# Two small constants move to the top of the left side of SBUF: every large tile on the left starts 64 bytes lower

## The chip, the cores and the metric

The kernel runs on one core of one Trainium2 chip. The metric is the device time of one execution in microseconds. Three runs of the kernel before took 1053.03, 1053.21 and 1053.92 us, so the median is 1053.21 us. The execution that the hardware profiler recorded took 1053.37 us, and the span from its first to its last instruction is 1051.6 us.

## The reference

One decoder block is computed on 1024 tokens of width 1024, in float32: a pre-norm, an input projection that feeds eight heads of forgetting attention and eight groups of chunked spatial gating, an output projection with a residual, and a gated MLP of width 2816 with a causal convolution of three taps between its two matrices, a second residual and a final norm.

```python
xn = rmsnorm(h, norm_mix_g)
proj = xn @ w_in
q, k, v = proj[..., :512], proj[..., 512:1024], proj[..., 1024:1536]
log_f = log_sigmoid(proj[..., 2560:] + b_forget)
att = forgetting_attention(q, k, v, log_f)      # softmax(q k' / 8 + c_i - c_j), causal
uv = gelu(proj[..., 1536:2560])
sg = chunked_spatial_gating(u, vg, gmlp_norm_g, w_spatial, b_spatial)
h = h + concat(att, sg) @ w_out
h = h + conv_ffn(rmsnorm(h, norm_ffn_g), w_up, conv_w, conv_b, w_down)
return rmsnorm(h, norm_final_g)
```

## The kernel before, in words

Every large matrix product is cut in four by a scheme with seven block products instead of eight, whose blocks have names such as A11, S2 and T3, B22. Each float32 operand is split in a high and a low part of type float32r (`split_w`, lines 480 to 487: ACT makes the high part, DVE subtracts it to get the low part), and each product is three float32r matmuls. Nearly all of them are 128x512: 128 rows, 128 columns of the stationary operand, 512 columns of the moving one.

The program has these stages in time: the products of the input projection for u, v and the gate (line 588, to about 104 us), those for q and k (line 737, to about 190 us), the spatial gating and the attention with the output projection of the gated half mixed in (lines 1046 to 1226, to about 380 us), the output projection of the attention and the second norm (lines 1464 to 1500), 22 units of the up projection with convolution and gate (line 1555, about 415 to 836 us), and the down projection with the final norm (line 1743, about 836 to 1044 us).

The order of the work on each engine is not written by hand. A class `Pace` records the instructions, knows which tile lies where in SBUF, gives each a cost, and lists them by due time; the order that it finds is then fixed on each engine. What it knows of places comes from `extent`, which adds up the sizes of the pools of one side from the bottom (left) or from the top (right).

SBUF is used as two stacks of pools. On the left, from the bottom up: `cst` (constants that live to the end), `sml` (small results of the attention), `early` (the tiles of the stages up to the attention: V, H0 to H3, x1, x2, t2, t3, wy, gg). When `early` is released, the pools `upl` (moving blocks xB11, xB21, xT2, xT3, the ring `wha`, the ring `sg`), `xtp`, `pst` and `dn` take its place. On the right, from the top down: `raws` (raw weights) and `late` (A, G0 to G3, pt, whl), later `upr` (xT1, xT4, xB22 and the ring `whb`). The left stack ends at byte 135136 of each partition, where the right one begins: all of it is in use.

The lines that the prediction names are these. Line 533 (ACT) and line 534 (DVE) split the first x tiles: those from tiles H read from byte 32 of the tile on, those from tiles V from byte 0. Line 616 (DVE) subtracts two x tiles. Line 814 is the matmul of the forget gate, whose stationary operand is a slice of 64 columns (256 bytes) of a tile `w` and whose moving operand is an x tile. Lines 1046, 1125 and 1500 are transposes on TensorE, with the constant `ident` as the moving operand. Lines 1555 and 1743 are the matmuls of the up and the down projection. Line 446 is the warm-up.

The two constants of the change are these:

- `lim`, 128x1 float32: set to 3e38 (line 448) and read as the first scalar of the running minimum in the attention (line 1112).
- `bcol`, 64x2 float32: the bias of the forget gate and its negative, read by the small operations of `forget` and `forget_sums`.

Of the kernel before, what the change touches and what calls it, by code (L numbers as in the profile page):

```python
# [8 lines left out]
F32 = mybir.dt.float32  # L9
# [5 lines left out]
P = 128  # L15
# [365 lines left out]
def block_kernel(ctx: ExitStack, tc: tile.TileContext, xT, xtok, wuv, wuw, wv, wqk, wf, cpk, xg, bfv,  # L381
# [3 lines left out]
    pace = Pace(tc)  # L385

    cst = pace.pool(ctx.enter_context(tc.tile_pool(name="cst", bufs=1)))
    sml = pace.pool(ctx.enter_context(tc.tile_pool(name="sml", bufs=1)), ring=4)
    early = pace.pool(tc.alloc_tile_pool(name="early", bufs=1))
    raws = pace.pool(tc.alloc_tile_pool(name="raws", bufs=1, side="right"), "right")  # L390
    late = pace.pool(tc.alloc_tile_pool(name="late", bufs=1, side="right"), "right")
    drm = ctx.enter_context(tc.tile_pool(name="drm", bufs=1, space=bass.MemoryType.DRAM))
# [43 lines left out]
    bs = cp[:, C_BS:C_BS + 8]  # L436
    eo = cst.tile([P, 2], F32, name="eo")
    eps, one = eo[:, 0:1], eo[:, 1:2]
    lim = cst.tile([P, 1], F32, name="lim")
    dve.memset(eps, EPS)  # L440

    warm = nc.const_aps.tensor(1.0, [P, 512], BF16)
# [17 lines left out]
    ng1 = cst.tile([P, 8], F32, name="ng1")  # L460
    rstd1 = cst.tile([P, 8], F32, name="rstd1")
    ss1 = cst.tile([P, 8], F32, name="ss1")
    bcol = cst.tile([64, 2], F32, name="bcol")


    qd = drm.tile([8, 2, 64, 1024], F32, name="qd")
# [923 lines left out]
        wo_split(3, hf, "pool")  # L1390
    ss2 = cst.tile([P, 8], F32, name="ss2")

    early.release()
    upl = pace.pool(tc.alloc_tile_pool(name="upl", bufs=1, reuse_waits="tile"))
    xtp = pace.pool(tc.alloc_tile_pool(name="xtp", bufs=1, reuse_waits="tile"))
# [560 lines left out]
```

## Time and profile before

| What | Value |
|---|---|
| median of three runs | 1053.21 us |
| the profiled execution | 1053.37 us |
| its span | 1051.6 us |
| PE busy | 1044.4 us, 99% of the span |
| DVE busy | 922.5 us, 88% |
| ACT busy | 575.4 us, 55% |
| POOL busy | 251.1 us, 24% |
| DMA, all queues | 158.24 MB, mean 150 GB/s |

PE stands for the matmuls of TensorE, PEld for the loads of its stationary operand, DVE for VectorE, ACT for ScalarE and POOL for GpSimd. [...]

### The profile page before, as it was taken

The page shows a single profiled execution, that of the slowest core. Times are in us where ns is not written, and L with a number is a line of the kernel's source. Part 1 is how long each engine was busy: PE and PEld are TensorE (multiplying, and loading weights), DVE is VectorE, ACT ScalarE, POOL GpSimd, SP SyncE. Part 2 cuts the span into 40 slices and gives each one's busy share as a digit, 9 for nine tenths or more (in the row PEclk, how much of TensorE's full clock was granted, in tenths as well). Part 3 has the DMA queues.
Part 4 walks back from the last instruction along what each step waited for, and adds up shares of the span by engine and source line. Part 5 has one row for each costly group of instructions (what it writes and reads, how often), then busy time and mean ns, then how long its engine had stood idle before and what let it go on. Part 6 is the DMA issues. An engine that isn't in the chain of part 4 may idle for free.

```text
span 1051.6 us, 14304 instructions
## 1 busy us (share of the span) xinstructions
PE 1044.4 (99%) x4925; PEld 866.3 (82%) x4925; DVE 922.5 (88%) x1389; ACT 575.4 (55%) x1007; POOL 251.1 (24%) x212
## 2 busy tenths in 40 slices
PE   9999999999999999999999999999999999999997
PEld 7888788888888888888888888888888888888886
DVE  6987999988888879999999999999998895697775
ACT  6658455477777756645444444444444454454653
POOL 0002243233362250073342433424322000000000
PEclk9999999999999999999999999999999999999999
DMA  9243267865664454214223331332323995333352
GB/s 341 92 149 100 73 183 235 267 213 160 224 208 141 141 186 175 80 66 146 101 90 131 100 138 63 116 125 73 133 75 102 346 388 202 94 98 99 95 180 90
DMA packets 65322, 158.24 MB, mean 150 GB/s; under 512 B 7697, under 2 KB 8537, under 8 KB 65249
## 3 DMA queue, kind: packets, MB, share of 16 engines
q1 hardware_dynamic: 64816, 156.50, 44.7%
q8 instruction: 39, 0.64, 0.3%
q10 hardware_dynamic: 432, 0.82, 0.2%
q14 instruction: 35, 0.28, 0.1%
HBM read 114.98 MB, written 42.31 MB: 150 GB/s over the span
## 4 chain that ended last, share of the span: by engine, by line
PE 99%; DVE 1%; ACT 0%; issue 0%
PE s L1555 23%; PE b L1555 17%; PE s L1743 11%; PE b L1743 9%; PE s L588 6%; PE b L588 5%; PE fl L1226 4%; PE s L737 4%; PE po L1147 3%; PE b L737 3%; PE tr L1125 3%; PE lg L1105 2%; PE lg L1104 2%; PE b L1466 1%; PE b L1465 1%; PE b L1464 1%
## 5 line engine op out<-in xcount | busy, mean ns | idle before, releaser
L1555 PE MATMUL s<-xT,whb 128*128 128x512 f32 x804 | 189.4, 389 | 0.0
L1555 PEld LDWEIGHTS s<-xT,whb 128*128 128x128 f32 x804 | 151.0, 188 | 31.3
L1555 PE MATMUL b<-xB,wha 128*128 128x512 f32 x528 | 126.9, 389 | 0.0
L1743 PE MATMUL s<-whb,wha 128*128 128x512 f32 (+1 forms) x528 | 118.9, 387 | 0.0
L1555 PEld LDWEIGHTS b<-xB,wha 128*128 128x128 f32 x528 | 99.0, 188 | 20.4
L1743 PEld LDWEIGHTS s<-whb,wha 128*128 128x128 f32 x528 | 98.5, 188 | 20.2
L481 ACT CAST whb<-sg 128x512 fp32r<-128x512 f32 x82 | 50.7, 618 | 91.8 <-PE s L1555 82.4
L481 ACT CAST wha<-sg 128x512 fp32r<-128x512 f32 x77 | 47.9, 622 | 92.3 <-PE b L1743 42.1
L1743 PE MATMUL b<-whb,wha 128*128 128x512 f32 (+1 forms) x408 | 91.8, 386 | 0.0
L1743 PEld LDWEIGHTS b<-whb,wha 128*128 128x128 f32 x408 | 75.9, 188 | 15.4
L487 DVE TENSOR_TENSOR wha<-sg,wha 128x512 fp32r<-128x512 f32 x77 | 52.9, 687 | 40.2 <-ACT wha L481 40.1
L1444 POOL TENSOR_TENSOR sg<-raw,raw 128x512 f32<-128x512 f32 x20 | 33.8, 1688 | 162.1 <-DVE whb L487 162.1
L1226 PE MATMUL fl<-whl,H 128*128 128x512 f32 x192 | 63.9, 407 | 0.0
L1147 PE MATMUL po<-pt,V 128*64 128x256 f32 (+6 forms) x240 | 63.9, 343 | 0.0
L1555 PE MATMUL s<-xB,whb 128*128 128x512 f32 x264 | 63.6, 390 | 0.0
L1131 ACT CAST pt<-tr 128x512 fp32r<-128x512 f32 (+2 forms) x96 | 45.2, 478 | 31.8 <-PE tr L1125 20.1
L1555 PE MATMUL b<-xT,whb 128*128 128x512 f32 x252 | 60.7, 389 | 0.0
L487 DVE TENSOR_TENSOR whb<-sg,whb 128x512 fp32r<-128x512 f32 x82 | 57.7, 723 | 2.1 <-ACT whb L481 2.0
L1136 DVE TENSOR_TENSOR pt<-tr,pt 128x512 fp32r<-128x512 f32 (+1 forms) x96 | 52.1, 552 | 7.7 <-ACT pt L1131 7.1
L1555 PEld LDWEIGHTS s<-xB,whb 128*128 128x128 f32 x264 | 49.5, 188 | 10.6 <-DVE h L1626 0.3
L1442 POOL TENSOR_TENSOR sg<-raw 128x512 f32<-128x512 f32 x20 | 41.5, 2076 | 60.0 <-DMA raw<-wup 58.0
L1555 PEld LDWEIGHTS b<-xT,whb 128*128 128x128 f32 x252 | 47.3, 188 | 9.8
(381 smaller groups left out, 2306.9 us busy)
## 6 DMA issues: line engine op xcount, KB each, us to landing
raw<-wup SPq DMA_DIRECT2D x44, 512.0 KB, 3.7
sg<-hx SPq DMA_DIRECT2D x77, 256.0 KB, 2.7
hx<-hs SPq DMA_DIRECT2D x44, 256.0 KB, 3.6
hx<-ca SPq DMA_DIRECT2D x33, 256.0 KB, 2.3
xT<-wdn SPq DMA_DIRECT2D x28, 256.0 KB, 5.4
raw<-wqk SPq DMA_DIRECT2D x8, 512.0 KB, 3.9
kd<-G SPq DMA_DIRECT2D x16, 256.0 KB, 5.1
qd<-G SPq DMA_DIRECT2D x16, 256.0 KB, 3.6
```

The source lines that it names most:

```text
L481: act.copy(h, src)
L487: return eng.tensor_tensor(out=l, in0=src, in1=f32(h), op=ALU.subtract)
L588: pe.matmul(banks[m], xs(n, xi, k)[:, ms], w[:, wi, :], start=(first and k == 0 and c == 0), stop=(k == 3 and c == 2), skip_group_check=True)
L737: pe.matmul(ps, w[:, wi, ks], xs(n, xi, k), start=(first and c == 0), stop=(c == 11), skip_group_check=True)
L1131: act.copy(pt[:, 0, o:512], ps[:, o:512])
L1136: dve.tensor_tensor(out=pt[:, 1, o:512], in0=ps[:, o:512], in1=f32(pt[:, 0, o:512]), op=ALU.subtract)
L1147: pe.matmul(po[0:n, c:e], lhs[:, 0:n], pt[:, s, c:e], start=(k == 0 and s == 0), stop=(k == 4 * hf + 3 and s == 1), skip_group_check=True)
L1226: pe.matmul(self.bank, sgT[k][:, xi, ts_], self.w[hf, k][:, wi, :], start=(k == 0 and i == 0), stop=(k == 3 and i == 2))
L1442: pool.tensor_tensor(out=s[0], in0=a21, in1=a22, op=ALU.add)
L1444: pool.tensor_tensor(out=s[2], in0=a21, in1=a11, op=ALU.add)
L1555: pe.matmul(ps, w[:, wi, ks], xb[:, xi, k, :], start=(first and n == 0), stop=(n == 11), skip_group_check=True)
L1743: pe.matmul(banks[bk + m if at is None else at][:, cs], xh[:, xi, ms], wh[:, wi, cs], start=((first and p_ == 0 or at == 0 and p_ == NP - ...
```

## The change

A pool `tiny` is opened on the left, on top of `early`. `lim` and `bcol` are taken from it instead of from `cst`, and it is released just ahead of `early`. Each of the two takes 32 bytes of a partition, so everything above `cst` on the left lies 64 bytes lower, and what lies in `cst` between and above the two lies 32 or 64 bytes lower.

| Tile | start before (modulo 512) | start now (modulo 512) |
|---|---|---|
| `lim` | 1952 (416) | 135072 (416) |
| `bcol` | 3360 (288) | 135104 (448) |
| `ident` | 1984 (448) | 1952 (416) |
| first tile of `early`, V; later xB11 | 4064 (480) | 4000 (416) |
| every other large tile on the left | (480) | (416) |
| x data within H0, first and second row | (0) and (32) | (448) and (480) |
| first tile of `late`, G0 | 135136 (480) | 135136 (480) |
| every other large tile on the right | (480) | (480) |

The instructions of each engine, their order, their shapes, and the semaphores and values that they wait for and raise are the same in both programs; what differs are the addresses of the operands on the left. Large tiles are multiples of 512 bytes long, so all tiles of a side share one remainder.

```diff
@@ -387,6 +387,7 @@
     cst = pace.pool(ctx.enter_context(tc.tile_pool(name="cst", bufs=1)))
     sml = pace.pool(ctx.enter_context(tc.tile_pool(name="sml", bufs=1)), ring=4)
     early = pace.pool(tc.alloc_tile_pool(name="early", bufs=1))
+    tiny = pace.pool(tc.alloc_tile_pool(name="tiny", bufs=1))
     raws = pace.pool(tc.alloc_tile_pool(name="raws", bufs=1, side="right"), "right")
@@ -436,7 +437,7 @@
-    lim = cst.tile([P, 1], F32, name="lim")
+    lim = tiny.tile([P, 1], F32, name="lim")
     dve.memset(eps, EPS)
@@ -460,7 +461,7 @@
-    bcol = cst.tile([64, 2], F32, name="bcol")
+    bcol = tiny.tile([64, 2], F32, name="bcol")
@@ -1390,6 +1391,7 @@
     ss2 = cst.tile([P, 8], F32, name="ss2")
 
+    tiny.release()
     early.release()
     upl = pace.pool(tc.alloc_tile_pool(name="upl", bufs=1, reuse_waits="tile"))
```

## Prediction

> **What bounds the kernel now.** I read the page's head and the engine shares of its chain first, to see which engine sets the end.
>
> ```profile
> span 1051.6 us, 14304 instructions
> PE 1044.4 (99%) x4925; PEld 866.3 (82%) x4925; DVE 922.5 (88%) x1389; ACT 575.4 (55%) x1007; POOL 251.1 (24%) x212
> PE 99%; DVE 1%; ACT 0%; issue 0%
> ```
>
> TensorE is busy for 1044.4 of 1051.6 us and makes 99% of the chain that ended last. Next I read the waits of PE, to see whether anything else ever holds it up.
>
> ```profile
> PE s L446 <- PEq L1948: 0.8, 1, 0.8
> PE b L1046 <- DVE mn L1112: 0.5, 1, 0.5
> ```
>
> Between its first and its last matmul PE waits once, for 0.5 us. So a time can change in two ways only: the step from one matmul to the next changes, or another engine becomes so late that PE has to wait. The chain in order of time gives the step (start, length, line, number of instructions).
>
> ```profile
> 27.58 21.76 PE b L588 x96
> 474.19 5.44 PE b L1555 x24
> 504.11 5.44 PE s L1555 x24
> 866.10 29.92 PE s L1743 x132
> ```
>
> 21.76/96, 5.44/24 and 29.92/132 are all 0.2267 us: every 128x512 matmul takes 226.7 ns in every large stage. That holds for different places of the operands. At line 588 the moving operand (a ring of weights) is mostly on the right and the stationary one on the left; at line 1743 likewise; at line 1555 into `b` with xB both are on the left, and into `s` the stationary one is on the right with the moving one on either side. But in all of these both streams start at 480 modulo 512, so these rows do not say what another remainder would do.
>
> The other engine to watch is DVE, in the up projection (length, then busy time and instructions of PE, PEld, DVE, ACT, POOL):
>
> ```profile
> 430.00:650.00 220.00, 220.00 (x972) 182.21 (x972) 215.63 (x232) 103.25 (x146) 84.84 (x48) 1.00 0.32 109
> ```
>
> DVE has 4.37 us left of 220, or 18.8 ns for each of its 232 instructions. It is covered, but thinly.
>
> **The change part by part.** No instruction, wait or order changes; no DMA is added. The change is that operands on the left start 64 bytes lower. I cost it by engine.
>
> *DVE, ACT.* The trace has pairs of equal operations whose source starts at another remainder: reading from H they start at 0 and 32 modulo 512, reading from V at 480 (minimum, median, maximum in ns).
>
> ```profile
> L533 ACT ACTIVATE x<-V,g x4: 723/724/726, 11.4 to 15.9; 128x512 fp32r<-128x512 f32 x4
> L533 ACT ACTIVATE V<-H,g x3: 724/724/725, 6.8 to 10.0; 128x512 fp32r<-128x512 f32 x3
> L534 DVE SCALAR_TENSOR_TENSOR x<-V,g,x x4: 751/751/752, 12.1 to 16.6; 128x512 fp32r<-128x512 f32 x4
> L534 DVE SCALAR_TENSOR_TENSOR V<-H,g,V x3: 750/752/752, 7.5 to 10.8; 128x512 fp32r<-128x512 f32 x3
> ```
>
> 724 against 724 ns on ACT, 751 against 752 ns on DVE, with the output at 480 in both. So an operation with one operand 32 or 64 bytes out of step costs at most 1 ns more or less: 232 times 1 ns is 0.2 us in those 220 us, against 4.37 us of cover. Cost: 0. If the cover were gone, every further nanosecond per DVE instruction would cost 0.23 us there.
>
> *DMA.* The only place where PE's chain hangs on transfers is the start, where ACT waits for the x tiles in H, and the transfers of the first 30 us fill the queues (the last two numbers are the DMA share and GB/s).
>
> ```profile
>   DMA H<-xT: 1.5, 2
> 0.00:30.00 30.00, 29.17 (x118) 22.25 (x119) 20.34 (x35) 19.43 (x32) 1.26 (x9) 1.00 0.95 348
> H<-xT SPq DMA_DIRECT2D x3, 256.0 KB
> ```
>
> Those targets move from 0 and 32 to 448 and 480 modulo 512. All other loads to tiles that start at 480 run in the same share of 0.95, so I take no difference; the bound on either side is a share of the 1.5 us of waiting, say a fifth, 0.3 us. [...]
>
> *PE.* This is the part without a row. First its size. At the very end the kernel has twelve 128x256 matmuls in a row, with their loads:
>
> ```profile
> 1044.05 1.51 PEld L1743 LDWEIGHTS b<-whb,wha 128*128 128x128 f32 x12
> L1743 PEld LDWEIGHTS b<-whb,wha 128*128 128x128 f32 x408 | 75.9, 188 | 15.4
> ```
>
> Twelve loads take 1.51 us and one takes 0.188, so the step is (1.51 - 0.188)/11 = 0.120 us. 256 columns more cost 226.7 - 120.2 = 106.5 ns, or 0.416 ns a column; 512 columns then need 213 ns, and 13.7 ns of each matmul do not depend on the columns. That is the most that a better start address could give back. The code has 4208 matmuls of 128x512: 1536 with the moving operand right and the stationary left, 776 the other way round (together 2312 mixed pairs), 912 with both left, 984 with both right.
>
> Is the 13.7 ns a matter of where the stream starts? If SBUF were read in blocks of 64, 128, 256 or 512 bytes, a stream of 2048 bytes from 480 touches 33, 17, 9 or 5 blocks; from 416 it touches 33, 17, 9 or 5 as well. One extra block of 128 bytes is 32 columns, 13.3 ns, which would fit the 13.7 ns, but then old and new start pay it alike. As the nearest row for two streams out of step I take the forget gate, whose stationary slices start at 480 and at 224 in turn while the moving operand stays at 480.
>
> ```profile
> L814 PEld LDWEIGHTS s<-x,whl x16: 133/134/135, 110.7 to 117.4; 128*64 128x64 f32 x16
> L814 PE MATMUL s<-x,whl x16: 387/393/397, 111.0 to 117.6; 128*64 128x512 f32 x16
> L1555 PE MATMUL s<-xT,whb 128*128 128x512 f32 x804 | 189.4, 389 | 0.0
> ```
>
> All 16 loads lie within 2 ns, whichever slice they read, and the matmuls spread by 10 ns around 393, against 389 at line 1555. The 4 ns may come from the narrower slice; as a price for being out of step, 0 and 4 ns are the two ends from this row. I take 0, because the loads do not tell the two starts apart.
>
> *ident.* It moves from 448, a multiple of 64, to 416, which is none. It is the moving operand of the transposes:
>
> ```profile
> 212.83 0.87 PE b L1046 x8
> L1500 PE MATMUL s<-ident,xn 128*128 128x128 f32 x64 | 8.9, 274 | 0.0
> ```
>
> 0.87/8 is 109 ns a transpose, while a stream of 128 columns needs 128 x 0.416 + 13.7 = 67 ns. [...] Cost: 0.
>
> Sum: 1053.37 us, the profiled execution, plus 0. That execution lies 0.16 us above the median of the three runs, so the forecast is 1053.2 us.
>
> **The rivals.** A measurement of this kernel tells about 0.2%, 2.1 us, from no change; the forecast's own range is therefore 1051.1 to 1055.3 us.
>
> A, *the two read streams get out of each other's way, faster.* If the 13.7 ns come from the stationary and the moving stream starting at the same remainder, the 2312 mixed pairs, now 64 bytes apart, lose up to all of it: 2312 x 13.7 = 31.7 us. With half of it, 1053.2 - 15.8 = 1037.4 us. For it: 13.7 ns do exist, and all pairs are in step today. Against it: line 814 with 256 bytes between its streams is no quicker. [...]
>
> B, *a longer first piece, faster.* From 480 a stream has 32 bytes (8 columns) ahead of the next 512-byte boundary, from 416 it has 96 (24 columns). If the matmul stalls at that boundary until the next piece is there, 16 columns more cover 6.7 ns of the stall. That helps the 776 + 912 = 1688 matmuls that move a left tile: 11.3 us, 1041.9 us. For it: it would explain a constant part. Against it: nothing in the trace separates it from a fixed cost.
>
> C, *the streams get into each other's way, slower.* If equal remainders are what keeps the two reads apart, the 2312 mixed pairs pay. At the 4 ns of line 814 that is 9.2 us, 1062.4 us; at another 13.7 ns it is 1084.9 us. It decides from 2.1/2312 = 0.9 ns a matmul on. For it: 393 against 389 ns. Against it: 64-column slices differ in more than the start.
>
> D, *DVE becomes the bound in the up projection, slower.* Operations with operands on both sides would have to take over 18.8 ns longer. At 40 ns, 232 instructions lose 232 x 21 ns = 4.9 us: 1058.1 us. The rows of lines 533 and 534 speak against it.
>
> That the change does not do what it says is excluded by the layout: the left tiles do start at 416.
>
> **How the numbers follow.** No change 0.76; A 0.09, B 0.05, C 0.08, D 0.02. Faster is A and B, 0.14; slower is C and D, 0.10. A, B and C get more than their rows give them because the one engine that counts has no row with its moving operand at another remainder. The range must hold 8 in 10: the forecast's own range has 0.76, and small forms of A, B (a gain of 1.5 ns on 2312 pairs is 3.5 us) and of C (1.2 ns, 2.8 us) make up the rest, so 1049.7 to 1056.0 us.
>
> **What would show it.** Right: the pieces of the chain at lines 588, 1555 and 1743 still read 226.7 ns, the first two rows of ACT and DVE still 724 and 751 ns, and DVE in 430 to 650 us about 215.6 us. A or C: the step changes at lines 1743 and 588 (mixed) and in half of line 1555, but not where both operands are left, `b` with xB at line 1555. B: it changes for all xB and for xT2 and xT3, not at line 1743. D: PE waits for DVE appear in the up projection. [...] A changed step of 128x512 matmuls is what would make the prediction wrong.

## The result and the profile after

The median went from 1053.57 us (1053.03 to 1054.22) to 1064.03 us (1063.77 to 1065.5), four runs of each kernel. The ratio on record is 1.0105 [1.0093, 1.0118] (the two medians alone give 1.0099): the change makes the kernel 10.5 us slower. The forecast of 1053.2 us was wrong, and 1064.03 us lies above its range. It is the place and the sign of rival C, which was given 1062.4 us and a chance of 0.08.

The profiled execution of the changed kernel took 1065.5 us, with 1.7 us outside its span. First its page's head, the engine shares of its chain, and all waits of PE:

```profile
span 1063.8 us, 14304 instructions
PE 1055.7 (99%) x4925; PEld 865.9 (81%) x4925; DVE 923.7 (87%) x1389; ACT 575.9 (54%) x1007; POOL 250.3 (24%) x212
PE 97%; DMA 1%; DVE 1%; ACT 0%; issue 0%; SPq 0%; DVEq 0%; ACTq 0%
...
PE s L447 <- PEq L1950: 0.8, 1, 0.8
PE b L589 <- ACT V L534: 0.7, 1, 0.7
PE s L1557 <- DVE h L1628: 0.5, 1, 0.5
```

PE is busy 11.3 us longer (1055.7 against 1044.4) over the same 4925 instructions, and the other four engines are within 1.2 us of before. PE still waits for next to nothing. So PE did not wait for anything: its own step became longer. The chain in order of time shows by how much (start, length, line, number of instructions):

```profile
28.96 22.00 PE b L589 x96
...
478.34 5.53 PE b L1557 x24
489.42 5.48 PE s L1557 x24
...
508.74 5.48 PE s L1557 x24
...
846.28 30.21 PE b L1745 x132
```

The kernel before has, for the last of them:

```profile
836.18 29.92 PE b L1743 x132
```

Where every one of these pieces had 226.7 ns a matmul, they now have 229.2, 230.4, 228.3, 228.3 and 228.9 ns. The names tell more. In the view by line, the same groups of the kernel before and of the changed one (minimum, median and maximum of a duration, first and last start; a duration is longer than the step, 389 ns against 226.7: in the traces the next matmul starts before this one ends):

```profile
L1555 PE MATMUL b<-xT,whb x252: 389/389/389, 433.7 to 822.0; 128*128 128x512 f32 x126
...
L1555 PE MATMUL b<-xB,wha x528: 387/389/476, 415.9 to 827.4; 128*128 128x512 f32 x176
...
L1743 PE MATMUL b<-whb,wha x408: 279/389/389, 836.0 to 1045.5; 128*128 128x512 f32 x132, 128*128 128x256 f32 x4
```

```profile
L1557 PE MATMUL b<-xT,whb x252: 392/394/398, 437.3 to 831.3; 128*128 128x512 f32 x126
...
L1557 PE MATMUL b<-xB,wha x528: 387/389/476, 419.4 to 836.9; 128*128 128x512 f32 x176
...
L1745 PE MATMUL b<-whb,wha x408: 276/392/394, 846.1 to 1057.6; 128*128 128x512 f32 x132, 128*128 128x256 f32 x4
```

Each of the 252 matmuls that stream a left xT against a stationary slice on the right is slower: the quickest now takes 392 ns, where all had 389. Where both operands are left (xB with wha) the median has not moved.

From the first start of each stage's line in the two traces, the stages compare so:

| Stage | before, us | after, us | difference |
|---|---|---|---|
| projections, line 588 now 589 | 98.88 | 101.06 | +2.2 |
| projections with the gates, 737 now 738 | 104.10 | 106.06 | +2.0 |
| from line 1046, now 1047, with the attention | 151.77 | 151.16 | -0.6 |
| output projection, 1464 now 1466 | 56.46 | 56.39 | -0.1 |
| up projection, 1555 now 1557 | 420.10 | 426.74 | +6.6 |
| down projection to PE's last start, 1743 now 1745 | 209.48 | 211.46 | +2.0 |

And from start to start of all matmuls of 128x512 in the two traces, by the sides of their operands:

| Moving, stationary | count | before, mean ns | after, mean ns | sum, us |
|---|---|---|---|---|
| right, left | 1536 | 230.5 | 232.1 | +2.50 |
| left, right | 776 | 227.2 | 233.6 | +4.96 |
| right, right | 984 | 228.5 | 230.8 | +2.20 |
| left, left | 912 | 231.3 | 234.0 | +2.49 |

That is 12.1 us in this execution, which is also 1.5 us above the median of the four. 0.5 us of the pairs on the right are the wait for DVE in line 1557. About 1.2 us of the pairs on the left stand at the start: the first group of line 588 that reads whl against V began at 11.10 us and now begins at 12.30 us, behind the 0.7 us of waiting for ACT. The three profiled kernels whose x data lie at 448 and 480 (this one and two of those below, with both sides at 416 and with other constants) begin that group at 12.30, 11.83 and 12.29 us, the other four between 10.87 and 11.28 us. With one execution of each, that is a hint that the new places of the x data delay the start, and not a proof; the kernel with both sides at 416 is as fast as before all the same. Without these two pieces, 7.5 us on the mixed pairs and 3.0 us on pairs of one side are left, 10.5 us, which is the difference of the medians. The split itself rests on one execution of each kernel.

### The profile page after: what moved, and what is told of

It is laid out like the page before. It is cut to its first block, busy times and chain, and to the rows that moved or that the text cites. A ratio compares the mean times of both kernels' runs of the same rounds, so it can differ in the third digit from the quotient of the medians.

```text
span 1063.8 us, 14304 instructions
## 1 busy us (share of the span) xinstructions
PE 1055.7 (99%) x4925; PEld 865.9 (81%) x4925; DVE 923.7 (87%) x1389; ACT 575.9 (54%) x1007; POOL 250.3 (24%) x212
## 4 chain that ended last, share of the span: by engine, by line
PE 97%; DMA 1%; DVE 1%; ACT 0%; issue 0%; SPq 0%; DVEq 0%; ACTq 0%
PE s L1557 22%; PE b L1557 17%; PE s L1745 11%; PE b L1745 9%; PE s L589 6%; PE b L589 5%; PE fl L1227 4%; PE s L738 4%; PE po L1148 3%; PE b L738 3%; PE tr L1126 3%; PE lg L1106 2%; PE lg L1105 2%; PE b L1468 1%; PE b L1467 1%; PE b L1466 1%
## 5 line engine op out<-in xcount | busy, mean ns | idle before, releaser
L1557 PE MATMUL s<-xT,whb 128*128 128x512 f32 x804 | 192.2, 392 | 0.0
L1557 PEld LDWEIGHTS b<-xT,whb 128*128 128x128 f32 x252 | 47.2, 187 | 11.3
```

The lines of the kernel that those rows point to most:

```text
L1557: pe.matmul(ps, w[:, wi, ks], xb[:, xi, k, :], start=(first and n == 0), stop=(n == 11), skip_group_check=True)
```

## The experiments

The question was what in the new addresses makes the step longer. Three theories were on record. **One:** only the distance between the start of the moving and the start of the stationary operand counts; it was 0 everywhere and is now 64 bytes (moving right, stationary left) or 448 (the other way). **Two:** a start at 416 is slow in itself. **Three:** it comes from the constants that moved, or from ident, which came off a multiple of 64. In all full kernels below the order, the waits and the semaphores are those of before; only addresses differ.

### A scan of the distance alone

The kernel leaves the whole block out; it runs 48 matmuls of 128x512 (float32r, as in the kernel) on each source line, back to back, with the moving operand a and the stationary one b bytes behind a multiple of 512. It ran once. The code is shortened:

```
def each(a, b, cols=512, wcols=128, ...):      # 48 in a row
    m0 = a // 4 + 512 * (1 if r % 3 == 2 else 0)
    w0 = b // 4 + 512 * (1 if r % 3 == 1 else 0)
    yield bk[0:wcols, 0:cols], wt[:, w0:w0 + wcols], mt[:, m0:m0 + cols]
for o, w, m in each(64, 0): pe.matmul(o, w, m, ...)
```

> A small kernel that leaves the whole block out: it loads four tiles of x, runs 48 float32r matmuls of 128x512 on each of some 42 lines, each line with its own start of the moving and of the stationary operand modulo 512 bytes, and stores x tiles as output. Theory 1 (only the distance between the two starts counts, modulo 512): all lines with equal starts (0/0, 480/480, 416/416, 448/448, 256/256) step at 226.7 ns, 10.88 us a line; moving 416 with stationary 480 at about 233.3 ns, 11.2 us; moving 480 with stationary 416 at about 229.3 ns, 11.0 us; the same distances at base 0 (448 and 64) give the same two numbers. Theory 2 (a start at 416 is bad by itself): 416/416 is at 229 ns or more, and a distance of 64 from base 0 stays at 226.7. Theory 3 (the moved constants are the cause, not the tiles): every line steps at 226.7 ns.

Its chain in order of time. The lines shown have distance 0, 32, 64, 128, 192, 256 and 448 with b at 0 (L44 to L58); then a and b both 480 (L68), 416 against 480 (L69), 480 against 416 (L70), both 416 (L71); then distance 0 with 256 columns (L74), a stationary slice of 64 columns at distance 0 (L76) and at 256 (L82), and distance 448 with 256 columns (L83).

```profile
24.14 10.88 PE bank L44 x48
35.02 11.20 PE bank L45 x48
46.22 11.00 PE bank L46 x48
...
68.43 11.20 PE bank L48 x48
...
90.87 11.19 PE bank L50 x48
...
113.25 10.88 PE bank L52 x48
...
179.99 11.19 PE bank L58 x48
...
292.06 10.92 PE bank L68 x48
302.98 11.20 PE bank L69 x48
314.18 11.20 PE bank L70 x48
325.38 10.93 PE bank L71 x48
...
358.14 5.75 PE bank L74 x48
...
372.21 11.04 PE bank L76 x48
...
422.26 11.04 PE bank L82 x48
433.31 5.46 PE bank L83 x48
```

At distance 0 a matmul takes 10.88/48 = 226.7 ns, the step of the kernel before. At 64 bytes it is 11.00/48 = 229.2, and at 32, 128, 192 and 448 it is 233.1 to 233.3 ns. **At 256 bytes it is 226.7 ns again.** The whole scan in steps of 32 bytes repeats after 256, not after 512. And 416 is not slow: with both operands there (L71) a matmul takes 227.7 ns including the change from the line before, and 226.7 once that is over. Theory two falls here. No distance is quicker than 0, so nothing of rival A is left either. One row missed what was expected of it: moving 480 against stationary 416 (L70), 64 bytes apart, was to take 11.0 us as L46 does and took 11.20; the second scan below takes this up.

L76 and L82 answer the row on which the prediction rested: with a stationary slice of 64 columns, distance 0 and distance 256 cost the same, 11.04/48 = 230.0 ns. Line 814 compared just these two.

Two lines behind L71 show one thing more. L72 has both operands at 448 and L73 both at 256:

```profile
336.31 10.91 PE bank L72 x48
347.21 10.92 PE bank L73 x48
```

Both have distance 0, and the group ahead of each has distance 0 too, at another start. Yet they take 0.03 and 0.04 us more than L44: their first seven and ten steps are uneven (L72: 230, 225, 230, 236, 229, 232, 231 ns), and then 226.7 ns is back. A change of start from one group to the next is enough for that.

### Both sides at 416

```diff
+    tinr = pace.pool(tc.alloc_tile_pool(name="tinr", bufs=1, side="right"), "right")
-    lim = cst.tile([P, 1], F32, name="lim")
+    lim = tinr.tile([P, 1], F32, name="lim")
-    bcol = cst.tile([64, 2], F32, name="bcol")
+    bcol = tinr.tile([64, 2], F32, name="bcol")
```

The same two constants move, but to the top of the right side, so that everything on the left and on the right starts at 416, ident too. Only the distance is as before.

> The two constants go to the top of the right side instead of the top of the left one, so that left and right tiles both start at 416. Theory 1 (distance between the two read streams): 226.7 ns a step again in every large stage, 1053.5 us as before. Theory 2 (416 itself is slow): all pairs suffer, not only those with a left operand, 1064 us or more. Theory 3 (the constants or ident at their new places): 1064 us, since lim and bcol have moved and ident is at 416 here too.

1053.0 us in ten runs against 1053.0, ratio 1.0 [0.9991, 1.0009]. Its chain:

```profile
474.29 5.44 PE b L1556 x24
```

5.44/24 is 226.7 ns. Taking the distance away takes the whole loss away, with the constants gone from their pool, ident at 416 and the x data at 448 and 480 all kept.

### Other constants, the same distance

```diff
+    tiny = pace.pool(tc.alloc_tile_pool(name="tiny", bufs=1))
-    ng1 = cst.tile([P, 8], F32, name="ng1")
+    ng1 = tiny.tile([P, 8], F32, name="ng1")
-    ss1 = cst.tile([P, 8], F32, name="ss1")
+    ss1 = tiny.tile([P, 8], F32, name="ss1")
```

The left goes to 416 again, but lim and ident keep their places. bcol stays in its pool; as it lies above ng1 and ss1 there, it too is 64 bytes lower, at 3296 (224 modulo 512), which the expectation overlooks.

> lim and bcol stay where they were; two other constants of 32 bytes, ng1 and ss1, go on top of the early tiles instead, so the left tiles start at 416 as in the change while ident keeps its start at 448. Theories 1 and 2: 1064 us, as the change. Theory 3 (lim, bcol or ident): 1053.5 us.

1063.96 us, ratio 1.0105 [1.009, 1.012], the loss of the change itself; its chain has the changed kernel's piece at line 1745:

```profile
845.26 30.21 PE b L1745 x132
```

With the run before, theory three falls: the loss is there when lim and ident stay and bcol is not taken out of its pool, and is not there when all three move and the distance stays 0.

### Distance 256

```diff
-    below = cst.tile([64, 64], F32, name="below")
+    below = tiny.tile([64, 64], F32, name="below")
```

below has 256 bytes of a partition, so the left tiles start at 224 and the right ones at 480.

> The 256-byte constant below goes on top of the early tiles, so the left tiles start at 224, ident at 448 as before. Theory 1: mixed pairs are now 256 bytes apart and step at a number of their own, not 226.7 ns; if every distance other than 0 costs what 64 costs, 1064 us; the run also says whether some distance is quicker than 0 (the forget gate of the kernel before, at 256 half of the time, stepped at 230 ns on average, which would give 1053.5 + 2312 x 3.3 ns = 1061 us). Theory 2: a number that depends on 224 alone. Theory 3: 1053.5 us.

1053.03 us in ten runs, ratio 1.0001 [0.9992, 1.0011].

```profile
473.69 5.44 PE b L1557 x24
...
865.37 29.92 PE s L1745 x132
```

The expectation of a step of its own, 1061 or 1064 us, was wrong: it took the period for 512 bytes. The full kernel agrees with the scan, 256 bytes apart is as good as together.

### Finer distances, what came before, and another type

A second kernel that leaves the block out: 36 matmuls at each distance from 0 to 252 in steps of 4, with 24 at distance 0 ahead of each; then pairs in different orders; then bfloat16 operands at seven distances. It too ran once.

> The small kernel again, which leaves the whole block out. Distances from 0 to 252 bytes in steps of 4, 36 matmuls of 128x512 each, with 24 matmuls at distance 0 ahead of each; then 64 and two pairs of lines after different forerunners; then bfloat16 operands at seven distances. Theory 1, as the first scan has it (period 256 bytes, best at 0): no distance lies under 226.7 ns, 64 is near 229 ns, most others at 231 to 238 ns. Rival: some distance that is no multiple of 32 bytes is quicker than 226.7 ns, and the kernel leaves time on the table at distance 0. On forerunners: if the step depends on the distance alone, both lines of moving 480 with stationary 416 show 229 ns; if it also depends on where the loads stood when the line began, they differ (233.3 ns was seen once). The 24 matmuls at distance 0 after a line at another distance: 226.7 ns from the first on if nothing is carried over, several at 224 to 236 ns if it is. For bfloat16, half the bytes a column, the collision theory expects a smaller or no effect; no number.

From its chain: distance 0 (L48), 20 (L57) and 64 (L79); behind another group at distance 0, moving 480 against stationary 416 (L181), 416 against 480 (L182), 480 against 416 once more (L183), and distance 0 (L184).

```profile
35.96 5.44 PE bank L48 x24
...
96.82 8.61 PE bank L57 x36
...
249.37 8.26 PE bank L79 x36
...
962.06 11.00 PE bank L181 x48
973.06 11.20 PE bank L182 x48
984.26 11.20 PE bank L183 x48
995.46 5.49 PE bank L184 x24
```

No distance is quicker than 226.7 ns; the best others settle at 228.8 to 229.0 (12, 28, 60, 64, 76, 108, 236), the worst at 240.0 (20, 68, 100, 116, 132, 196, 244). Two more things are to be seen. L181 and L183 are the same pair of starts, and take 229.2 and 233.3 ns: which of the two holds depends on what ran before. Not every forerunner does it: 64 against 0 behind twelve matmuls of 416 against 480 (L179) has 229.2 ns too. And a group at distance 0 behind a group at another distance is not back at once: the 24 matmuls of L184 take 5.49 us, 228.7 ns each, of which the last twelve have 226.7. Over all distances such a group averages 226.7 to 229.6 ns (5.44 to 5.51 us).

The bfloat16 lines, from the view by time (start, length; one record of the 48 is missing in each):

```profile
1011.16 10.52 PE L186 MATMUL bank<-movb,wtsb 128*128 128x512 bf16 x47
...
1062.96 10.52 PE L191 MATMUL bank<-movb,wtsb 128*128 128x512 bf16 x47
```

From L186 to L191 there are five lines of 48: 51.80/240 = 215.8 ns each, at distances 32, 64, 128, 192 and 256 alike. Among these bfloat16 lines the distance makes no difference, and a step is 10.9 ns shorter than the 226.7 ns of float32r at distance 0.

### Distances 128 and 192 in the full kernel

The scan says which distances are dear, so the full kernel should follow. For the left at 352 (128 bytes apart both ways), lim, ng1, rstd1 and bcol move; for the left at 32 (448 where the moving operand is right, 64 where it is left, the reverse of the change), g1, lim, below, ng1, rstd1, ss1 and bcol:

```diff
-    rstd1 = cst.tile([P, 8], F32, name="rstd1")
+    rstd1 = tiny.tile([P, 8], F32, name="rstd1")
```

> Four constants of 32 bytes (lim, bcol, ng1, rstd1) on top of the early tiles: left tiles start at 352, 128 bytes below the right ones. Theory 1 with the steps of the first scan: a distance of 128 costs 233.3 ns in both directions, so 2312 mixed pairs lose 6.6 ns each, 15.3 us, and the same-side pairs beside them some 4 us as they did in the change: 1072 us. If the loss grew with the number of bytes moved, it would be twice that of the change, 1074 us, which this run alone does not tell apart from it; the run at 256, which lost nothing, does.

> 448 bytes of constants (below, lim, bcol, ng1, rstd1, ss1, g1) on top of the early tiles: left tiles start at 32, so the distance is that of the change with its sign turned (448 below is 64 above, modulo 512). Theory 1: the pairs that move a left operand (776) are now at 64, 1.6 ns each, 1.2 us, and those that move a right one (1536) at 448, 6.4 ns each, 9.8 us; with 4 us on same-side pairs 1068 us, that is 4 us more than the change although the constants that move are no more than that. If the sign does not matter, 1064 us.

The left at 352 gave 1066.99 us, ratio 1.0134 [1.0118, 1.0149]; the left at 32 gave 1065.56 us, ratio 1.0122 [1.0105, 1.0139]. The order is as expected, but both are 2 to 5 us quicker than that. The down projection, where every matmul moves a right tile against a left one, in the chain of the first and of the second:

```profile
844.23 30.67 PE b L1745 x132
```

```profile
841.84 30.80 PE b L1745 x132
```

That is 232.3 and 233.3 ns a matmul, where the change has 228.9 and before 226.7: in this long run of equal pairs the full kernel has the steps of the scan to within 1 ns (233.3 for 128 and 448, 228.9 for 64). The expectation was too high in three places. It let all 1536 pairs of that kind pay: 240 of them stand at lines 1147 and 1226 of the kernel before, where matmuls of different shapes alternate, had lost the even step already (248.6 and 244.5 ns on average from one start to the next), and lose 1 to 2 ns in these two runs. At 352 the long runs step at 232.3 ns and not at 233.3. And groups of one side pay behind mixed ones, but less than the 4 us assumed: in the up projection of both runs xB with wha goes from 227.1 to 229.1 ns, 1.1 us for its 528 matmuls, and xB with whb on the right only from 227.3 to 227.5. Both together, against the scan's prices on the mixed pairs alone (settled steps less 226.7 ns):

| Left at | 1536 pairs, moving right | 776 pairs, moving left | scan's sum, us | measured, us |
|---|---|---|---|---|
| 416 | 2.2 ns | 6.7 ns | 8.6 | 10.5 |
| 32 | 6.7 ns | 2.2 ns | 12.0 | 12.5 |
| 352 | 6.7 ns | 6.7 ns | 15.5 | 13.9 |
| 224 | 0 | 0 | 0 | 0.0 |

The scan gives the order and the size to within 2 us, not the digit.

## Why the prediction was wrong

**The step that failed** is the price of PE: "as a price for being out of step, 0 and 4 ns are the two ends from this row. I take 0, because the loads do not tell the two starts apart." The stationary slices of line 814 lie 0 and 256 bytes from the moving start. The scan has a period of 256 bytes, and with 64-column slices it has 230.0 ns at both (and at 64 bytes even less, 228.3 ns, where 128 columns take more than at 0). The row could not have shown an effect that is there; equal rows were read as the absence of one. The second reason, that a stream from 416 touches as many blocks of 64, 128, 256 or 512 bytes as one from 480, looked at one stream, while the cost is between two: both operands at 416 cost nothing (1053.0 us, 5.44/24 = 226.7 ns a matmul). That the memory is read in blocks at all was the author's assumption, and no run shows it. In place of the 0 the changed kernel pays, per mixed pair, 1.6 ns where the moving operand is right and 6.4 ns where it is left, and some 3 us beside them on pairs of one side.

**The 4 ns** (393 against 389 ns) at line 814 belong in the main to the narrow slice, as was suspected: the scan has a step of 230.0 against 226.7 ns for 64 columns at distance 0.

**Rival C** was right in place, sign and nearly in size: 2312 mixed pairs at 4 ns, 9.2 us. Measured on these pairs in the profiled execution are 7.5 us. That 9.2 us came so near is luck: the 4 ns were those of the narrow slice, and say nothing of a distance. Its reason against, that the narrow slices differ in more than the start, was true, and no reason against C. What was missing in it is the other part, some 3 us on pairs of one side. The place where it arises is to be seen in the up projection of the changed kernel (view by time; start, length, tiles, number):

```profile
500.23 2.96 PE L1557 MATMUL b<-xT,whb 128*128 128x512 f32 x12
503.03 2.96 PE L1557 MATMUL s<-xT,whb 128*128 128x512 f32 x12
505.83 2.91 PE L1557 MATMUL b<-xB,wha 128*128 128x512 f32 x12
508.58 0.62 PE L1557 MATMUL s<-xT,whb 128*128 128x512 f32 x2
```

From start to start, the two groups with xT on the left against whb on the right take 2.80 us, 233.3 ns a matmul, which is the scan's price for 448. The group behind them has both operands left and yet takes 2.75 us, 229.2 ns. The single steps there, in ns from start to start in the trace, for this group (left) and the next one (right):

```
b<-xB,wha   236 224 231 236 228 233 231 226 227 227 226 226
s<-xT,whb   228 230 233 236 224 231 236 228 232 231 227 227 226 227 227 ...
```

In this stretch each change of side is followed by three to ten uneven steps before the even 227, 227, 226 is back, unless a mixed group follows, which has 233.3 ns at once; before the change no such steps were there. So a pass of 84 matmuls, 24 of them mixed, takes 19.32 us (489.42 to 508.74 in the chain) instead of 84 times 226.67 ns, 19.04. Of the 0.28 us, 24 x 6.6 = 0.16 are on the mixed pairs and 0.12 on the others. It is the behaviour of L184 in the second scan, where an even rhythm, once lost, comes back only after some ten matmuls. The second group loses it again with both its operands on one side, as L72 and L73 of the first scan do: the change of start ahead of it is enough. What happens in that change was not tried apart. One candidate: the load for the first matmul of the second group runs from 508.36 to 508.55 us, within the matmul before it, which runs from 508.35 to 508.74 us and whose moving operand is of the other side. No run shows that this is the cause.

**Rivals A and B** fall with the scan. No distance goes below 226.7 ns, and both operands at 416, with a longer first piece, are no quicker. The 13.7 ns that a matmul has beyond its columns are real (120.0, 173.3 and 226.7 ns for 256, 384 and 512 columns at distance 0 in the scan, 13.3 ns beyond 0.4167 ns a column), but no start gives them back. B's 512-byte boundary and stall were the author's assumption, and no run shows them.

**A reading that was too wide.** "every 128x512 matmul takes 226.7 ns in every large stage" holds for the long runs of equal matmuls at lines 588, 737, 1555 and 1743, and not between lines 1046 and 1464: the 192 of line 1226, for one, have 244.5 ns on average from their start to the next. This does not change the forecast, but the pairs there lose less than the others.

**Right: DVE and ACT.** The rows that were to stay did, at lines that are now 534 and 535:

```profile
L534 ACT ACTIVATE x<-V,g x4: 722/724/726, 12.3 to 16.8; 128x512 fp32r<-128x512 f32 x4
...
L534 ACT ACTIVATE V<-H,g x3: 722/725/726, 8.3 to 11.0; 128x512 fp32r<-128x512 f32 x3
```

```profile
L535 DVE SCALAR_TENSOR_TENSOR x<-V,g,x x4: 751/752/752, 13.1 to 17.5; 128x512 fp32r<-128x512 f32 x4
...
L535 DVE SCALAR_TENSOR_TENSOR V<-H,g,V x3: 751/752/752, 9.1 to 11.7; 128x512 fp32r<-128x512 f32 x3
```

Medians moved by 1 ns at most. DVE's busy time in 220 us of the up projection (second column PE, then PEld, DVE):

```profile
434.00:654.00 220.00, 220.00 (x958) 179.42 (x958) 213.93 (x229) 101.66 (x142) 85.51 (x48) 1.00 0.31 108
```

213.93 us for 229 instructions is 0.934 us each, against 215.63/232 = 0.929 before; PE is busy for all 220 us and only fits 958 matmuls instead of 972. Rival D did not happen.

**Right: ident and the transfers.** In the time of the whole kernel both cost nothing that can be measured: with ident at 416 and the x data at 448 and 480 the kernel with both sides at 416 takes 1053.0 us. No row of the kernel before shows the 0 for ident. The chain of the changed kernel, with ident at 416, has eight transposes in the same 0.87 us that eight took at line 1046:

```profile
216.22 0.87 PE b L1047 x8
```

What sets these 109 ns a transpose is not shown. The first matmul of line 588 starts at 4.71 us against 4.70; the later start of the group behind it is told above and stays open.

**What was to show it.** "A or C: the step changes at lines 1743 and 588 (mixed) and in half of line 1555, but not where both operands are left" was the right place to look. Its last part holds for the median (389 ns before and after) and not for the group's sum, because of the matmuls behind a mixed group.

**The chances.** 0.76 for no change rested on one row without power. The prediction said itself that the one engine that counts has no row with its moving operand at another remainder. With PE at 99% of the chain, 0.9 ns a matmul was enough to be measured, and the other end that the prediction named, 4 ns, deserved about as much as its 0.

## What to carry to other kernels

When a kernel is bound by float32r matmuls of 512 columns, keep the moving and the stationary operands' starts equal modulo 256 bytes (226.7 ns a matmul in these runs, against 228.8 to 240.0): if the two come from different sides of the memory, a small constant added or moved on one side alone shifts all pairs across the sides, here for 1%. After any edit of the layout, read the step of a long run of matmuls from the chain before anything else. And before a row of equal numbers is taken as "no effect", ask whether the effect would have shown in it: two starts that differ by a whole period, here 256 bytes, say nothing.

## What the runs showed of the hardware

- In a run of equal float32r matmuls of 128x512, one costs 226.7 ns when its two operands start equally modulo 256 bytes, and 228.8 to 240.0 ns otherwise (multiples of 4 bytes were tried); 32, 96, 128, 192 and 224 bytes settle at 233.3 ns, 64 at 228.9 behind matmuls at distance 0. bfloat16 operands have 215.8 ns at every distance that was tried.
- The step depends on what ran before: the same pair of starts took 229.2 ns behind matmuls at distance 0 and 233.3 ns behind 48 with the two starts exchanged. Behind a group with other starts, the even step of 226.7 ns is back at once in some cases and after up to eleven matmuls in others; between two groups of distance 0 at different starts it took seven and ten.
- For 256 columns the sign turns: distance 0 takes 5.75/48 = 119.8 ns (120.0 once settled) and 448 takes 5.46/48 = 113.8 ns (113.3). With 384 columns all four distances that were tried have 173.3 ns. The full kernel was not changed for this; its long stages have 512 columns.
- In these runs PE's time depends on how the starts of its own two operands lie to each other, by up to 13.3 ns on 226.7.
- What lies behind it stays open: why the period is 256 bytes, why 64 is milder than 192, and why the steady step depends on the past. The runs show the dependence on the two starts and not the parts of the chip that meet there. No layout was found that is faster than the kernel before; distance 0 is its own, and 256 equals it (1053.03 us, ratio 1.0001).
